# Places and order of the operand differences ahead of the MLP, and of one weight sum at the start of its down projection, in a hybrid SSD/attention layer

## The chip, the core and the metric

The kernel runs on one core of a Trainium2 chip. The core has a matrix engine (TensorE; PE in the profile, with its weight loads as PEld), a vector engine (DVE), a scalar engine (ACT), GpSimd (POOL) and SyncE (SP), each with its own queue of instructions, taken in order. POOL and SP also issue DMAs. The metric is the device time of one launch in microseconds (us); less is better.

## The reference

The reference is one layer of a streaming encoder: an RMS norm, a combined input projection, a Mamba-2 SSD group and a forgetting-attention group, an output projection, and then an MLP. There are 1152 tokens of width 1024 (1024 of a prompt and 8 x 16 of running streams). The change bears on the MLP only, whose hidden width is 4096:

```python
def trunk_layer(x, conv_prev, ssm_prev, fox_fn, norm1_w, w_in, ...):
...
    x = x + jnp.einsum("ble,ed->bld", mix, w_out)
    h = rms_norm(x, norm2_w)
    x = x + jnp.einsum("blf,fd->bld", jnp.square(jax.nn.relu(jnp.einsum("bld,df->blf", h, w_up))), w_down)
    return x, (k, v, logf, ssm_state, conv_state)
```

## The kernel before

**Float32 by parts.** A float32 operand is split into a high part (a copy by ACT into the matmul's format) and a low part (operand minus high part, on DVE). One product is then three matmuls: high weight by high operand, high weight by low operand, low weight by high operand. Every operand thus costs one ACT and one DVE instruction before PE can use it. A buffer that holds both parts is a *place*; part A's places are called XA10 to XA71, part B's XB10 to XB71, by the operand's number (1, 2, 5, 6, 7, 3, 4) and a half (0 or 1).

**Strassen.** Most of the MLP multiplies 2 x 2 blocks with seven products instead of eight. A product takes a sum or difference of weight blocks (`weights`, from line 1203, which yields them in the order 1, 2, 5, 6, 7, 3, 4) and a sum or difference of operands (`operand`, line 1170). `s1` (line 1210) is the weight sum of product 5, `s2` (L1213) that of product 6, `a21` (L1215) the difference of product 7 and `a12` (L1217) that of product 3. `parts` (L1199 on ACT, L1200 on DVE) splits a weight. Weights arrive by DMA from SP (`raws`, L1192) in the three buffers `wraw` and the two `a22`; their parts lie in four buffers `w`.

**The up projection** (`mlp`): hidden blocks f = 0 and 1 are multiplied plainly by `up_plain`, here called the first and the second, while the operands of the others are still being made; f = 2 to 15 follow with seven products each (`up`), of 24 matmuls each. The second's weights lie in four places of part A that are not yet taken (XA51, XA61, XA70, XA71). `chain("B", ...)` makes B's first operands of the third token block; its last low part is `made_b`. Then `operand` forms the differences of operands 5, 6, 7 and 4 (L1178), eight for each part, in place in the buffers of the normed activations (x20, xh, xl, g3), and splits them (L1180 on ACT, L1181 on DVE). After their products, `up_plain` forms the Strassen combinations of its hidden values (`hidden_out`, L1253), which POOL puts to DRAM (`Hd`, L1250); they lie in `ts`, two places of part B.

**The down projection** (`mlp_down`) goes through 19 steps (q, a, b): output block q, hidden blocks a to b. Step 0 takes two hidden blocks (12 matmuls in a product), step 1 three (18) and step 2 four (24). The hidden operands come back from `Hd` by POOL's DMAs (L1393) and are split by `hidden_parts` (L1401 on ACT, L1402 on DVE): 28 of them are split for the first four steps, 14 of these (f = 0 and 1) ahead of step 0. Results leave PSUM (tiles D, four of them) through DVE additions at L1429 and, for some, a copy at L1449.

**What sets the order.** A scheduler orders each engine's instructions by a simulation with priorities. `keep_in_program_order` pins instructions: all pinned ones of an engine keep the order in which the program writes them. `issue_after(x)` only holds an instruction behind x. `later` shifts a priority. So the order of an engine's queue, and not the program text alone, decides what waits for what.

Of the kernel before, what the change touches and what calls it, by code (L numbers as in the profile page):

```python
# [6 lines left out]
F32 = mybir.dt.float32  # L7
BF16 = mybir.dt.bfloat16
F32R = mybir.dt.float32r
I32 = mybir.dt.int32  # L10
AF = mybir.ActivationFunctionType
ALU = mybir.AluOpType
# [33 lines left out]
XB = 1  # L46
# [3 lines left out]
ORDER = (1, 2, 5, 6, 7, 3, 4)  # L50
# [13 lines left out]
class Trunk:  # L64
# [1098 lines left out]
        return [self.place(part, i, j, F32R) for j in range(2)]  # L1163

    def place(self, part, i, j, dt):
        return self.t(self.xap if part == "A" else self.xbp, [P, 2, 2, TC], dt, f"X{part}{i or 4}{j}")

    def operand(self, part, i, X):


        nc = self.nc
        b11, b12 = self.pieces(part, 0, 0), self.pieces(part, 0, 1)
        b21, b22 = self.pieces(part, 1, 0), self.pieces(part, 1, 1)
        src, minus = {1: (b11, None), 2: (b21, None), 0: (b12, None), 3: (b22, None),
                      5: (b11, (b12, b11)), 6: (b11, (b22, b11)), 7: (b12, (b22, b12)), 4: (b21, (b21, b11))}[i]
        for j in range(2):
            if minus is not None:
                self.tc.keep_in_program_order(nc.vector.tensor_tensor(src[j], minus[0][j], minus[1][j], op=ALU.subtract))  # L1178
            hi, lo = X[j][:, 0], X[j][:, 1]
            nc.scalar.activation(hi, src[j], AF.Copy)  # L1180
            nc.vector.tensor_tensor(lo, src[j], hi.bitcast(F32), op=ALU.subtract)  # L1181
# [18 lines left out]
        nc.vector.tensor_tensor(w[:, 1, 0:n], src, w[:, 0, 0:n].bitcast(F32), op=ALU.subtract)  # L1200
        return w

    def weights(self, load, n, raw=None, pin=lambda x: x):

        a11, a12, a21, a22 = self.raws(load, n, raw)
        v = self.nc.vector
        yield 1, self.parts(a11, n)
        yield 2, self.parts(a12, n)
        s1 = self.t(self.wr2, [P, 512], F32, "s1", 1)[:, 0:n]
        pin(v.tensor_tensor(s1, a21, a22, op=ALU.add))  # L1210
        yield 5, self.parts(s1, n)
        s2 = self.t(self.wr2, [P, 512], F32, "s2", 1)[:, 0:n]
        v.tensor_tensor(s2, s1, a11, op=ALU.subtract)  # L1213
        yield 6, self.parts(s2, n)
        pin(v.tensor_tensor(a21, a11, a21, op=ALU.subtract))  # L1215
        yield 7, self.parts(a21, n)
        v.tensor_tensor(a12, a12, s2, op=ALU.subtract)  # L1217
        yield 3, self.parts(a12, n)
        yield 4, self.parts(a22, n)
# [51 lines left out]
    def up_plain(self, f, A, B):  # L1271

        nc, I = self.nc, self.I
        halves = lambda part, i, dt: [self.place(part, i, j, dt) for j in range(2)]
        hb = [x[:, j] for x in halves("B", (6, 7)[f], F32) for j in range(2)]
        if f:
            ws = [x.rearrange("p a b t -> p (a b t)")[:, 0:1024].rearrange("p (a b) -> p a b", a=2)
                  for x in [self.place("A", i, 1, F32R) for i in (5, 6)] + halves("A", 7, F32R)]
        else:
            ws = [None] * 4  # L1280
        a = [self.parts(x, 512, w) for x, w in zip(self.raws(lambda ij: I["wu"][f, ij], 512, plain=True), ws)]
        for part, X in enumerate((A, B)):
            if f:
                groups = (((0, 0), (0, 1)), ((1, 0), (1, 1)))
            else:
                groups = (((0, 0), (1, 0)), ((0, 1), (1, 1)))
            for group in groups:
                banks = self.bank2()

                order = [(n, half, j) for half in range(2) for j in range(2) for n in range(2)]  # L1290
                if f:
                    order.sort()
                for n, half, j in order:
                    row, col = group[n]
                    ps = banks[:, n, 0:TC]
                    w, x = a[2 * row + half], X[((1, 2), (0, 3))[col][half]][j]
                    for k in range(2):
                        o = slice((2 * j + k) * P, (2 * j + k + 1) * P)
                        self.mm(ps, w[:, 0, o], x[:, 0, k], half == j == k == 0, False)
                        self.mm(ps, w[:, 0, o], x[:, 1, k], False, False)  # L1300
                        self.mm(ps, w[:, 1, o], x[:, 0, k], False, half == j == k == 1)
                    if half == j == 1:
                        h = hb[2 * row + col][:, part]
                        nc.scalar.activation(h, ps, AF.Relu)
                        nc.scalar.activation(h, h, AF.Square)
            yield
        ts = [x[:, j] for x in halves("B", 5, F32) for j in range(2)]
        for n in (0, 3, 1, 2):
            self.hidden_out(f, hb, ts, n)
        yield  # L1310
# [45 lines left out]
    def mlp(self):  # L1356
        XA, XB = self.XA, {}
        self.XB = XB
        self.late = []
        for i in (1, 2, 0, 3):  # L1360
            XB[i] = self.block("B", i)
        first, second = (self.up_plain(f, XA, XB) for f in range(2))
        next(first)
        next(second)
        with self.later(-1010000):
            rb, = self.norm2((2,))
            made_b = self.chain("B", ((2, (1, 2)),), {2: rb}, XB)
        for ins, tbs in ((self.made_a, (0, 1)), (made_b, (2,))):
            with self.tc.issue_after(ins.ins):
                for tb in tbs:  # L1370
                    self.scaled_rest(tb, self.room[:, tb, TB:TB + TB - TC] if tb < 2 else rb[:, TC:TB])
        for i in (0, 3):
            self.operand("B", i, XB[i])
        next(first)
        next(first)
        next(second)
        for i in (5, 6, 4, 7):
            XA[i] = self.block("A", i)
            self.operand("A", i, XA[i])
        next(second)  # L1380
        for i in (5, 6, 7, 4):
            XB[i] = self.block("B", i)
            self.operand("B", i, XB[i])
        for f in range(NC, NF):
            self.up(f)
# [9 lines left out]
    def hidden_parts(self, f, i):  # L1395

        nc = self.nc
        self.parted.add((f, i))
        h = self.hs[f, i]
        raw = h[:, 1].bitcast(F32)  # L1400
        nc.scalar.activation(h[:, 0], raw, AF.Copy)  # L1401
        nc.vector.tensor_tensor(h[:, 1], raw, h[:, 0].bitcast(F32), op=ALU.subtract)  # L1402

    def yrows(self, q, x):

# [72 lines left out]
        self.strassen(lambda ij: self.I["wd"][q, ij, :, ks], len(fs), rhs, ev, after, raw, **kw)  # L1478

    def mlp_down(self):  # L1480
        self.hs = {}
        steps = [(0, 0, 1), (1, 0, 2), (2, 0, 3), (3, 0, 3), (0, 2, 4), (1, 3, 5), (2, 4, 6), (3, 4, 7), (0, 5, 8), (1, 6, 9),
                 (2, 7, 10), (3, 8, 11), (0, 9, 12), (1, 10, 12), (2, 11, 13), (3, 12, 15), (0, 13, 15), (2, 14, 15), (1, 13, 15)]
        end = {f: n for n, (q, a, b) in enumerate(steps) for f in range(a, b + 1)}
        nc = self.nc
# [29 lines left out]
        for n, (q, a, b) in enumerate(steps):  # L1515
            def after(i):
                wait.append([])
                for f in range(NF - 4):
                    if end[f] == n:
                        self.hidden(f + 4, i)  # L1520
                        wait[-1].append((f + 4, i))
                if len(wait) > 4:
                    coming.extend(wait.pop(0))
                coming.sort(key=lambda fi: (begin[fi[0]], ORDER.index(fi[1])))
                for _ in range(2 if len(coming) > 3 else 1):
                    if coming:
                        self.hidden_parts(*coming.pop(0))

            kw = {}
            if n in (1, 2):  # L1530

                kw["pin"] = self.tc.keep_in_program_order
            if n == 1:
                kw["pre"] = lambda: self.load_y(1, nc.sync)
            self.down(q, list(range(a, b + 1)), n < 4, b == NF - 1, after, **kw)

# [250 lines left out]
```

## Time and profile before

| | us |
|---|---|
| three runs | 1685.35, 1692.79, 1697.54 |
| median | 1692.79 |
| the profiled execution, its own time | 1687.61 |
| its span in the trace | 1685.9 |

The busy shares in the page are 94% for PE, 75% for DVE, 47% for ACT and 29% for POOL. The MLP takes the time from about 955 us to the end of the span. In the views, a row gives a group of like instructions: start and duration in us, engine, line, operation, output and inputs, and their count; a bracket at its end is the engine's idle time ahead of the group, and what ended it. DMA issues are rows of the engine that issues them. Line numbers are those of the kernel before.

### The profile page before, as it was taken

The numbers are of one execution on the slowest core, as the hardware profiler recorded it, in microseconds if no ns is written. First come the engines' busy times: TensorE is split into PE (matmuls) and PEld (weight loads), VectorE is DVE, ScalarE is ACT, GpSimd is POOL, SyncE is SP. The second block draws the span as 40 slices with busy tenths as digits, with TensorE's granted clock in tenths as the row PEclk, the third lists the DMA queues.
The fourth block names the chain that finished last, engine by engine and source line by source line (L and its number), as shares of the span: only waits on it lengthen the run. The fifth ranks groups of instructions, "written<-read, shape, count | busy, mean of one in ns | idle before, by whom it ended". The sixth has DMA issues, their size and how long they took to land.

```text
span 1685.9 us, 29655 instructions
## 1 busy us (share of the span) xinstructions
PE 1591.1 (94%) x10709; PEld 1493.9 (89%) x10709; DVE 1262.4 (75%) x2336; ACT 788.9 (47%) x1573; POOL 483.9 (29%) x624
## 2 busy tenths in 40 slices
PE   8999999999898988999799989999999789999999
PEld 7999987889776867889689989999999689999998
DVE  7955676777777888795768787666668769888887
ACT  6322244446654444565754455445556224343431
POOL 1333322113654576333112012222225312111100
PEclk9999999999999999999999999999999899999999
DMA  7374477857889778965545244444447435344433
GB/s 232 100 206 118 117 216 249 288 161 216 258 265 285 211 246 254 295 188 161 162 159 167 69 138 154 144 149 149 143 143 273 153 98 181 114 142 140 148 119 105
DMA packets 193450, 299.75 MB, mean 178 GB/s; under 512 B 25592, under 2 KB 116520, under 8 KB 191256
## 3 DMA queue, kind: packets, MB, share of 16 engines
q1 hardware_dynamic: 133960, 183.60, 35.3%
q0 software_dynamic: 24240, 86.21, 15.7%
q10 hardware_dynamic: 35104, 28.06, 5.2%
q8 instruction: 85, 1.39, 0.3%
q14 instruction: 61, 0.50, 0.1%
HBM read 207.16 MB, written 90.63 MB: 177 GB/s over the span
## 4 chain that ended last, share of the span: by engine, by line
PE 67%; DMA 13%; DVE 12%; issue 3%; ACT 2%; SPq 2%; POOL 1%; ACTq 0%; DVEq 0%; POOLq 0%
PE D L127 41%; PE d L127 12%; PE o L127 4%; PE s L127 4%; PE c L127 2%; PE u L127 1%; DMA sb<-in_ssT 1%; DMA xb<-xbD 1%; DMA M<-acsTd 1%; DMA kt<-in_ckT 1%; DMA qb<-QS 1%; PE m L127 1%; DVE eh L702 1%; DVE qkv L305 1%; DMA wraw<-in_wq 1%
## 5 line engine op out<-in xcount | busy, mean ns | idle before, releaser
L127 PE MATMUL D<-XA,w 128*128 128x288 f32 x2616 | 404.4, 299 | 19.3 <-ACT w L1199 14.6
L127 PE MATMUL D<-XB,w 128*128 128x288 f32 x2616 | 399.5, 297 | 6.3 <-DVE XB L1181 4.0
L127 PEld LDWEIGHTS D<-XA,w 128*128 128x128 f32 x2616 | 369.3, 191 | 23.0 <-ACT w L1199 15.5
L127 PE MATMUL d<-xh,w 128*128 128x384 f32 x1344 | 370.9, 346 | 8.2 <-ACT xh L1003 2.6
L127 PEld LDWEIGHTS D<-XB,w 128*128 128x128 f32 x2616 | 366.6, 190 | 8.9 <-DVE XB L1181 4.7
L127 PEld LDWEIGHTS d<-xh,w 128*128 128x128 f32 x1344 | 245.9, 191 | 25.3 <-issue 10.1
L127 PE MATMUL d<-xl,w 128*128 128x384 f32 x672 | 231.7, 345 | 3.9 <-DVE xl L1004 3.7
L1199 ACT ACTIVATE w<-wraw 128x512 fp32r<-128x512 f32 (+2 forms) x132 | 78.4, 596 | 143.8 <-PE D L127 113.6
L123 POOL TENSOR_TENSOR w<-wraw,w 128x512 fp32r<-128x512 f32 x76 | 102.1, 1350 | 128.6 <-ACT w L121 125.0
L127 PEld LDWEIGHTS d<-xl,w 128*128 128x128 f32 x672 | 128.3, 191 | 11.9 <-DVE xl L1004 7.1
L121 ACT ACTIVATE w<-wraw 128x512 fp32r<-128x512 f32 x120 | 74.3, 627 | 93.5 <-PE d L127 50.3
L1200 DVE TENSOR_TENSOR w<-wraw,w 128x512 fp32r<-128x512 f32 (+2 forms) x132 | 84.6, 643 | 18.1 <-ACT w L1199 17.8
L1393 POOL DMA_DIRECT2D XA<-Hd x56 | 30.4, 542 | 166.3 <-PE D L127 128.4
L1199 ACT ACTIVATE w<-s 128x512 fp32r<-128x512 f32 (+2 forms) x66 | 39.0, 591 | 66.4 <-PE D L127 59.4
L1401 ACT ACTIVATE XB<-XB 128x576 fp32r<-128x576 f32 x56 | 37.9, 684 | 62.9 <-DMA XB<-Hd 62.6
L1401 ACT ACTIVATE XA<-XA 128x576 fp32r<-128x576 f32 x56 | 37.9, 683 | 52.0 <-DMA XA<-Hd 51.8
L127 PE MATMUL d<-wq,xh 128*128 128x384 f32 (+1 forms) x192 | 52.8, 351 | 7.5 <-ACT wq L121 6.7
L1402 DVE TENSOR_TENSOR XB<-XB 128x576 fp32r<-128x576 f32 x56 | 41.7, 751 | 21.7 <-ACT XB L1401 21.6
L1393 POOL DMA_DIRECT2D XB<-Hd x56 | 30.3, 541 | 91.1 <-PE D L127 70.4
L523 DVE SCALAR_TENSOR_TENSOR acc<-xr,cwh,acc 128x1024 f32<-128x1024 f32 x36 | 47.2, 1310 | 10.2 <-ACT acc L520 10.1
L127 PE MATMUL o<-wq,xh 128*128 128x384 f32 (+1 forms) x192 | 52.2, 347 | 0.0
L127 PE MATMUL s<-wq,xh 128*128 128x384 f32 (+1 forms) x192 | 52.1, 349 | 0.0
(572 smaller groups left out, 3223.5 us busy)
## 6 DMA issues: line engine op xcount, KB each, us to landing
Hd<-xl POOLq DMA_DIRECT2D x56, 288.0 KB, 4.3
XA<-Hd POOLq DMA_DIRECT2D x56, 288.0 KB, 3.3
XB<-Hd POOLq DMA_DIRECT2D x56, 288.0 KB, 3.7
wraw<-in_wch SPq DMA_DIRECT2D x56, 256.0 KB
wraw<-in_wu SPq DMA_DIRECT2D x50, 256.0 KB
wraw<-in_wos SPq DMA_DIRECT2D x48, 256.0 KB
M<-acsTd SPq DMA_DIRECT2D x18, 512.0 KB
kt<-in_ckT SPq DMA_DIRECT2D x8, 1024.0 KB
```

What stands on the lines that cost most here:

```text
L121: nc.scalar.activation(w[:, 0, :], raw, AF.Copy)
L123: eng.tensor_tensor(w[:, 1, :], raw, w[:, 0, :].bitcast(F32), op=ALU.subtract)
L127: self.nc.tensor.matmul(out, lhsT, rhs, start=start, stop=stop)
L305: nc.vector.tensor_tensor(v4, v4, rs[:, i, :].unsqueeze(2).to_broadcast([P, 4, 64]), op=ALU.mult)
L523: nc.vector.scalar_tensor_tensor(acc[:, 0:SEQ], xr[:, k:k + SEQ], cw[:, b, k:k + 1], acc[:, 0:SEQ], op0=ALU.mult, op1=ALU.add)
L702: nc.vector.tensor_tensor(eh[:, 1, w], ps[:, w], eh[:, 0, w].bitcast(F32), op=ALU.subtract)
L1199: nc.scalar.activation(w[:, 0, 0:n], src, AF.Copy)
L1200: nc.vector.tensor_tensor(w[:, 1, 0:n], src, w[:, 0, 0:n].bitcast(F32), op=ALU.subtract)
L1393: self.nc.gpsimd.dma_start(h[:, 1].bitcast(F32), self.Hd[f][:, (1, 2, 3, 5, 6, 7, 4).index(i)])
L1401: nc.scalar.activation(h[:, 0], raw, AF.Copy)
L1402: nc.vector.tensor_tensor(h[:, 1], raw, h[:, 0].bitcast(F32), op=ALU.subtract)
```

## The change

Four edits, none of which adds or takes away an instruction:

1. `place` crosses the places of part A's operands 5 and 6: operand 5 takes XA50 and XA60, operand 6 takes XA51 and XA61. The second's weights stay in XA51, XA61, XA70 and XA71.
2. The sixteen differences of `operand` are no longer pinned; each is only held behind `made_b`.
3. The second's `ts` are XB60 and XB61 instead of XB50 and XB51 (the first's `ts` stay in XB50 and XB51).
4. The sum `s1` and the difference `a21` of down steps 1 and 2 are no longer pinned. In step 1, `s1` is held behind the fourteenth low part of the hidden operands (`h_lo[13]`).

```diff
     def place(self, part, i, j, dt):
+        if part == "A" and i in (5, 6):
+
+            i, j = 5 + j, i - 5
         return self.t(self.xap if part == "A" else self.xbp, [P, 2, 2, TC], dt, f"X{part}{i or 4}{j}")
...
-                self.tc.keep_in_program_order(nc.vector.tensor_tensor(src[j], minus[0][j], minus[1][j], op=ALU.subtract))
+                with self.tc.issue_after(self.made_b.ins):
+                    nc.vector.tensor_tensor(src[j], minus[0][j], minus[1][j], op=ALU.subtract)
...
-    def weights(self, load, n, raw=None, pin=lambda x: x):
+    def weights(self, load, n, raw=None, behind=None):
...
-        pin(v.tensor_tensor(s1, a21, a22, op=ALU.add))
+        with ExitStack() as es:
+            if behind is not None:
+                es.enter_context(self.tc.issue_after(behind))
+            v.tensor_tensor(s1, a21, a22, op=ALU.add)
...
-        pin(v.tensor_tensor(a21, a11, a21, op=ALU.subtract))
+        v.tensor_tensor(a21, a11, a21, op=ALU.subtract)
...
-                  for x in [self.place("A", i, 1, F32R) for i in (5, 6)] + halves("A", 7, F32R)]
+                  for x in halves("A", 6, F32R) + halves("A", 7, F32R)]
...
-        ts = [x[:, j] for x in halves("B", 5, F32) for j in range(2)]
+        ts = [x[:, j] for x in halves("B", 5 + f, F32) for j in range(2)]
...
-            made_b = self.chain("B", ((2, (1, 2)),), {2: rb}, XB)
+            self.made_b = self.chain("B", ((2, (1, 2)),), {2: rb}, XB)
...
-        nc.vector.tensor_tensor(h[:, 1], raw, h[:, 0].bitcast(F32), op=ALU.subtract)
+        self.h_lo.append(nc.vector.tensor_tensor(h[:, 1], raw, h[:, 0].bitcast(F32), op=ALU.subtract))
...
-            if n in (1, 2):
-
-                kw["pin"] = self.tc.keep_in_program_order
             if n == 1:
+
+                kw["behind"] = self.h_lo[2 * len(ORDER) - 1].ins
                 kw["pre"] = lambda: self.load_y(1, nc.sync)
```

The changed file numbers its lines up to seven higher: L1178, L1181, L1200, L1210, L1213, L1215, L1217, L1253, L1320, L1402 and L1429 of before are L1182, L1185, L1204, L1217, L1220, L1222, L1224, L1260, L1327, L1409 and L1436 there; ACT's L1199, L1401 and L1449 are L1203, L1408 and L1456.

The instructions differ in order in two stretches only. The first is the start of the MLP. On DVE before, ahead of the first differences (x_1686 is x20; w_10750 and the next are the weights of f = 2; XB_1846 and XB_1847 are the first's ts in XB50 and XB51, XB_1858 is half of the second's; XA_1850 is the first half of operand 5):

```order
L1200 TENSOR_TENSOR w_10750<-wraw_10742,w_10750 128x512
L1200 TENSOR_TENSOR w_10780<-wraw_10744,w_10780 128x512
L1217 TENSOR_TENSOR wraw_10744<-wraw_10744,s_1884_10843 128x512
L1200 TENSOR_TENSOR w_10814<-s_1881_10812,w_10814 128x512
L1253 TENSOR_TENSOR XB_1846_10541<-XB_1812_10100 128x576
L1200 TENSOR_TENSOR w_10845<-s_1884_10843,w_10845 128x512
L1253 TENSOR_TENSOR XB_1846_10541<-XB_1813_10101,XB_1846_10541 128x576
L1253 TENSOR_TENSOR XB_1847_10542<-XB_1813_10101,XB_1812_10100 128x576
L1253 TENSOR_TENSOR XB_1847_10542<-XB_1813_10101,XB_1846_10541 128x576
L1178 TENSOR_TENSOR x_1686_9390<-xh_1601_8786,x_1686_9390 128x2x288
L1253 TENSOR_TENSOR XB_1858_10692<-XB_1824_10228 128x576
L1181 TENSOR_TENSOR XA_1850_10660<-x_1686_9390,XA_1850_10660 128x576
```

And the same place on DVE now, up to the same weight's low part (XB_1808 to XB_1811 are the last of B's plain operands, xl, xh and g are sources of differences):

```order
L1182 TENSOR_TENSOR xl_1602_8787<-g_1687_9391,xl_1602_8787 128x2x288
L1182 TENSOR_TENSOR xl_1603_8788<-g_1687_9391,xl_1603_8788 128x2x288
L1185 TENSOR_TENSOR XB_1808_10096<-g_1687_9391,XB_1808_10096 128x576
L1185 TENSOR_TENSOR XB_1809_10097<-g_1687_9391,XB_1809_10097 128x576
L1185 TENSOR_TENSOR XB_1810_10098<-g_1687_9391,XB_1810_10098 128x576
L1182 TENSOR_TENSOR xh_1601_8786<-xh_1601_8786 128x2x288 x2
L1185 TENSOR_TENSOR XB_1811_10099<-g_1687_9391,XB_1811_10099 128x576
L1185 TENSOR_TENSOR XA_1850_10660<-x_1686_9390,XA_1850_10660 128x576
L1185 TENSOR_TENSOR XA_1851_10661<-x_1686_9390,XA_1851_10661 128x576
L1182 TENSOR_TENSOR g_1687_9391<-g_1687_9391 128x576 x2
L1182 TENSOR_TENSOR x_1686_9390<-xh_1601_8786,x_1686_9390 128x2x288 x2
L1204 TENSOR_TENSOR w_10750<-wraw_10742,w_10750 128x512
```

Differences, and both low parts of operand 5 in part A, now stand ahead of the weights of f = 2; the differences used to begin behind the first's combinations.

The second stretch is the start of the down projection. On DVE before, around the sum of step 1 (XA_2251, XB_2252 and XB_2253 are the last of the 28 hidden operands; D_14447 and D_14473 are results of step 1; s_2281 is s1, s_2284 is s2; w_14495 and w_14520 are their parts):

```order
L1402 TENSOR_TENSOR XA_2251_14219<-XA_2251_14219 128x576
L1429 TENSOR_TENSOR x_2219_14147<-D_14447,x_2219_14147 128x576
L1402 TENSOR_TENSOR XB_2252_14221<-XB_2252_14221 128x576
L1402 TENSOR_TENSOR XB_2253_14223<-XB_2253_14223 128x576
L1429 TENSOR_TENSOR x_2219_14147<-D_14473,x_2219_14147 128x576
L1210 TENSOR_TENSOR s_2281_14493<-wraw_14432,a_2276_14434 128x384
L1213 TENSOR_TENSOR s_2284_14518<-s_2281_14493,wraw_14428 128x384
L1200 TENSOR_TENSOR w_14495<-s_2281_14493,w_14495 128x384
L1217 TENSOR_TENSOR wraw_14430<-wraw_14430,s_2284_14518 128x384
L1200 TENSOR_TENSOR w_14520<-s_2284_14518,w_14520 128x384
L1429 TENSOR_TENSOR x_2219_14147<-D_14498,x_2219_14147 128x2x576
L1429 TENSOR_TENSOR x_2219_14147<-D_14523,x_2219_14147 128x576
```

On DVE now, the place of the sum:

```order
L1436 TENSOR_TENSOR a_2225_14153<-D_14347,a_2225_14153 128x576
L1409 TENSOR_TENSOR XA_2239_14188<-XA_2239_14188 128x576
L1217 TENSOR_TENSOR s_2281_14493<-wraw_14432,a_2276_14434 128x384
L1409 TENSOR_TENSOR XB_2240_14197<-XB_2240_14197 128x576
L1409 TENSOR_TENSOR XB_2241_14199<-XB_2241_14199 128x576
L1204 TENSOR_TENSOR w_14436<-wraw_14428,w_14436 128x384
```

And on DVE now, what follows from the low part of w_14495 on:

```order
L1409 TENSOR_TENSOR XA_2250_14217<-XA_2250_14217 128x576
L1204 TENSOR_TENSOR w_14495<-s_2281_14493,w_14495 128x384
L1220 TENSOR_TENSOR s_2284_14518<-s_2281_14493,wraw_14428 128x384
L1409 TENSOR_TENSOR XA_2251_14219<-XA_2251_14219 128x576
L1436 TENSOR_TENSOR g_2218_14146<-D_14412,g_2218_14146 128x576
L1436 TENSOR_TENSOR x_2219_14147<-D_14447,x_2219_14147 128x576
L1222 TENSOR_TENSOR wraw_14432<-wraw_14428,wraw_14432 128x384
L1409 TENSOR_TENSOR XB_2252_14221<-XB_2252_14221 128x576
L1409 TENSOR_TENSOR XB_2253_14223<-XB_2253_14223 128x576
L1224 TENSOR_TENSOR wraw_14430<-wraw_14430,s_2284_14518 128x384
L1204 TENSOR_TENSOR w_14520<-s_2284_14518,w_14520 128x384
```

The sum has moved ahead of fourteen hidden low parts, directly behind the one of XA_2239, and its own low part ahead of the last three; the difference of product 7 (L1222) has moved ahead of two of them.

On ACT before, the high part of the sum stands behind all 28 copies and one result:

```order
L1401 ACTIVATE XA_2250_14217<-XA_2250_14217 128x576
L1401 ACTIVATE XA_2251_14219<-XA_2251_14219 128x576
L1401 ACTIVATE XB_2252_14221<-XB_2252_14221 128x576
L1401 ACTIVATE XB_2253_14223<-XB_2253_14223 128x576
L1449 ACTIVATE x_2219_14147<-D_14447 128x576
L1199 ACTIVATE w_14495<-s_2281_14493 128x384
L1199 ACTIVATE w_14520<-s_2284_14518 128x384
```

On ACT now:

```order
L1408 ACTIVATE XB_2249_14215<-XB_2249_14215 128x576
L1203 ACTIVATE w_14495<-s_2281_14493 128x384
L1408 ACTIVATE XA_2250_14217<-XA_2250_14217 128x576
L1408 ACTIVATE XA_2251_14219<-XA_2251_14219 128x576
L1408 ACTIVATE XB_2252_14221<-XB_2252_14221 128x576
L1408 ACTIVATE XB_2253_14223<-XB_2253_14223 128x576
L1203 ACTIVATE w_14520<-s_2284_14518 128x384
```

It stands ahead of the last four copies now, and the high part of w_14520 ahead of the result's copy.

More of the change, by code (lines that the diff above doesn't have):

```diff
@@ L1366, in mlp @@
             rb, = self.norm2((2,))
-            made_b = self.chain("B", ((2, (1, 2)),), {2: rb}, XB)
-        for ins, tbs in ((self.made_a, (0, 1)), (made_b, (2,))):
+            self.made_b = self.chain("B", ((2, (1, 2)),), {2: rb}, XB)
+        for ins, tbs in ((self.made_a, (0, 1)), (self.made_b, (2,))):
             with self.tc.issue_after(ins.ins):
@@ L1480, in mlp_down @@
     def mlp_down(self):
-        self.hs = {}
+        self.hs, self.h_lo = {}, []
         steps = [(0, 0, 1), (1, 0, 2), (2, 0, 3), (3, 0, 3), (0, 2, 4), (1, 3, 5), (2, 4, 6), (3, 4, 7), (0, 5, 8), (1, 6, 9),
```

## The prediction

> **What bounds the kernel now.** I read the span first, then the waits of PE, then busy time by stretches, and last the rows of the engines around the two stretches that the change reorders. Of the waits, grouped by what PE needed and what ended the wait (total us, times, longest), and of the busy time (stretch, length, then PE, PEld, DVE, ACT and POOL busy; then granted clock, DMA share, GB/s), these rows matter:
>
> ```profile
> span 1685.9 us, 29655 instructions
> PE D L127 <- ACT w L1199: 14.6, 4, 8.0
> PE D L127 <- DVE XB L1181: 4.0, 3, 2.9
> 985.00:1000.00 15.00, 10.31 (x45) 8.45 (x45) 14.83 (x23) 8.78 (x15) 0.74 (x1) 0.77 0.24 75
> 1320.00:1340.00 20.00, 11.84 (x61) 11.39 (x62) 12.91 (x21) 4.31 (x8) 1.58 (x3) 0.75 0.27 89
> 1360.00:1380.00 20.00, 17.83 (x121) 17.38 (x121) 12.56 (x18) 5.49 (x9) 1.10 (x2) 0.91 0.26 80
> 1380.00:1480.00 100.00, 100.00 (x756) 100.00 (x755) 88.51 (x138) 43.73 (x74) 19.37 (x36) 1.00 0.51 157
> ```
>
> PE is the bound: from 1380 to 1480 it is busy all the time at full clock. Time is lost where PE stands, and in the stretch at a lower granted clock behind it: 1320 to 1340 has 61 matmul records where 100 us at full pace have 756. Both places are the ones reordered, so the change is priced as PE time given back there. After either place PE runs full, so that what is saved stays saved, unless it is lost inside the place.
>
> **First stretch, start of the MLP (edits 1 to 3).** PE's rows:
>
> ```profile
> 982.35 2.69 PE L127 MATMUL D<-XA,w 128*128 128x288 f32 x19
> 988.43 0.40 PE L127 MATMUL D<-XB,w 128*128 128x288 f32 x1 [0.46 <-ACT XB L1180]
> 991.70 1.99 PE L127 MATMUL D<-XB,w 128*128 128x288 f32 x6 [2.87 <-DVE XB L1181]
> 994.37 1.57 PE L127 MATMUL D<-XB,w 128*128 128x288 f32 x5 [0.68 <-DVE XB L1181]
> 995.89 3.26 PE L127 MATMUL D<-XA,w 128*128 128x288 f32 x13
> 1010.11 1.77 PE L127 MATMUL D<-XA,w 128*128 128x288 f32 x12
> 1295.41 1.75 PE L127 MATMUL D<-XB,w 128*128 128x288 f32 x12
> 1297.00 1.76 PE L127 MATMUL D<-XA,w 128*128 128x288 f32 x12
> ```
>
> Full pace is the step from 1295.41 to 1297.00: 1.59 us for 12 matmuls, 0.1325 each. Product 5 of f = 2 begins at 982.35, product 5 of f = 3 at 1010.11; between them lie seven products of 24, 168 matmuls, worth 22.3 us. It takes 27.8, so 5.5 us are lost: the waits for part B's operands, and 13 matmuls in 3.26 us at low clock behind them. Why the operands are late shows on DVE:
>
> ```profile
> 963.71 1.49 DVE L1200 TENSOR_TENSOR w<-wraw,w 128x512 fp32r<-128x512 f32 x2 [5.18 <-ACT w L1199]
> 973.78 0.75 DVE L1178 TENSOR_TENSOR x<-xh,x 128x576 f32<-128x576 f32 x1
> 980.28 1.43 DVE L1253 TENSOR_TENSOR XB<-XB,XB 128x576 f32<-128x576 f32 x2 [0.72 <-ACT XB L1305]
> 990.89 0.75 DVE L1181 TENSOR_TENSOR XB<-xl,XB 128x576 fp32r<-128x576 f32 x1
> 993.57 0.75 DVE L1181 TENSOR_TENSOR XB<-xl,XB 128x576 fp32r<-128x576 f32 x1
> ```
>
> DVE stands for 5.18 us ahead of 963.71, waiting for a weight, and starts the sixteen differences only at 973.78. They are pinned to one another in alternation with low parts that wait for places held by the second's weights, so the low parts of XB51 and XB60 come at 990.89 and 993.57. In the changed order eight differences and both low parts of operand 5 in part A stand in that idle time: ten instructions of 0.67 us each (two in a train take 1.43, one 0.75) from 958.53, where the idle time begins, to 965.2. So the first weight's low part is 1.5 us later than at 963.71; its product lies 72 matmuls, 9.5 us, ahead of 982.35, which hides that. From 965.2 to the end of the low part of XB50 lie 13 instructions of 0.67 and six on weights of 0.75: 978.4, or about 981 if a combination waits for ACT as at 980.28. PE wants that part 12 matmuls into product 5, at 983.9.
>
> Edit 3 moves the second's combinations to XB60 and XB61, so that operand 6 of part B now waits for their way to DRAM, which operand 5 did before. Of the DMAs in 960 to 1000, and of those in the crowded stretch from 1270 to 1325 (KB each, median us from issue to landing), with POOL's last issue before:
>
> ```profile
> Hd<-XB POOLq DMA_DIRECT2D x13, 288.0 KB, 2.4
> XB<-Hd POOLq DMA_DIRECT2D x14, 288.0 KB, 7.0
> 984.01 0.54 POOL L1250 DMA_DIRECT2D Hd<-XB  x1 [1.46 <-DVE XB L1253]
> ```
>
> The last combination, issued at 984.01 before, ends five instructions of 0.67 and one of 0.75 behind 980.28, with its own 0.67 at 985.1; issued in 0.54 it goes out by 985.8 and lands at 988.2. PE wants the high part of XB61 about 92 matmuls after 982.35, at 994.5. Even a landing of 7.0 us leaves a margin of about one us after ACT's copy. So the whole loss of 5.5 us is taken as gain. The ends: 5.5, if nothing is late; and a loss of 2.5, if the landing takes twice the 7.0 and PE stands some 6.5 us, with 1.5 us of slow matmuls behind. I take 5.5, since the nearest row, of these same puts, is 2.4. PE's own reordered rows ahead of 982.35 and two weight loads that move on SP behind the copies of residual rows are covered by the same margins.
>
> **Second stretch, start of the down projection (edit 4).** PE, DVE, ACT and SP:
>
> ```profile
> 1315.51 2.39 PE L127 MATMUL D<-XB,w 128*128 128x288 f32 x16 [0.43 <-DVE w L1200]
> 1325.94 4.44 PE L127 MATMUL D<-XA,w 128*128 128x288 f32 x18 [8.04 <-ACT w L1199]
> 1330.22 0.97 PE L127 MATMUL D<-XB,w 128*128 128x288 f32 x6
> 1335.00 0.53 PE L127 MATMUL D<-XA,w 128*128 128x288 f32 x2 [2.22 <-ACT w L1199]
> 1352.68 0.53 PE L127 MATMUL D<-XA,w 128*128 128x288 f32 x2 [2.17 <-ACT w L1199]
> 1353.40 1.81 PE L127 MATMUL D<-XA,w 128*128 128x288 f32 x7 [0.20 <-DVE w L1200]
> 1363.47 0.53 PE L127 MATMUL D<-XA,w 128*128 128x288 f32 x2 [2.17 <-ACT w L1199]
> 1371.69 1.37 PE L127 MATMUL D<-XA,w 128*128 128x288 f32 x9
> 1309.83 0.75 DVE L1402 TENSOR_TENSOR XA<-XA 128x576 fp32r<-128x576 f32 x1
> 1320.05 0.75 DVE L1402 TENSOR_TENSOR XA<-XA 128x576 fp32r<-128x576 f32 x1
> 1324.72 0.55 DVE L1210 TENSOR_TENSOR s<-wraw,a 128x384 f32<-128x384 f32 x1
> 1325.92 0.56 DVE L1200 TENSOR_TENSOR w<-s,w 128x384 fp32r<-128x384 f32 x1
> 1333.49 0.55 DVE L1215 TENSOR_TENSOR wraw<-wraw,wraw 128x384 f32<-128x384 f32 x1
> 1309.65 1.25 ACT L1401 ACTIVATE XB<-XB 128x576 fp32r<-128x576 f32 x2
> 1337.16 0.63 ACT L1199 ACTIVATE w<-wraw 128x512 fp32r<-128x512 f32 x1 [1.39 <-DMA wraw<-in_wd]
> 1288.67 0.37 SPq L1192 DMA_DIRECT2D a<-in_wd  x1
> 1334.10 2.27 SPq L1192 DMA_DIRECT2D wraw<-in_wd  x3
> ```
>
> From the down projection's first product at 1297.00 to the last product of step 2 at 1371.69 lie 7 x 12, 7 x 18 and 6 x 24 = 354 matmuls, worth 46.9 us; it takes 74.7, so 27.8 us are lost. The sum of step 1 stands behind all hidden low parts, at 1324.72, and PE waits 8.04 us for its high part. Behind it 18 matmuls take 4.28 us, to 1330.22 (0.238 each, the low clock). The difference of product 7 waits for a result at 1333.49, and that frees the buffers of step 2's weights, so SP issues them at 1334.10, ACT has the first at 1337.16, and step 2 has two waits of 2.17 us of its own with slow matmuls behind them.
>
> In the changed order the sum is directly behind the low part at 1309.83, thus at 1310.50; it takes 0.47 and makes all behind it that much later (PE reaches product 5 at 1317.90 + 0.47 = 1318.4; 1317.90 is 1325.94 less the wait). ACT copies its high part behind the two copies begun at 1309.65, by 1311.6. Its low part stands behind the low part at 1320.05, which ends at 1320.72, or 1321.2 with the 0.47; it is there at 1321.8. PE does two matmuls, stands for about 3.2 us, and does the other 16 at 0.238: 1325.6. The low part of product 6's weight has ahead of it s2, three more instructions of 0.67, the difference of product 7 (0.47), the last two hidden low parts (1.34) and that of product 3 (0.47): it is there at 1327.0, 0.9 us after PE's second matmul of product 6. Everything else of step 1 is then on DVE ahead of PE, so that 70 matmuls run to 1336.3. Step 2's raw weights are issued when the difference of product 7 and the last uses of the buffers are through, at about 1325 to 1330, and land some three us later (1334.10 to 1337.16 before); its sum's parts are wanted at 1342.7. So step 2 runs through: 144 matmuls, to 1355.4. The gain is 1371.69 - 1355.4 = 16.3 us. The ends: 22.3, if PE never stands from 1318.4 on (234 matmuls, to 1349.4); 4.7, if only the low part is earlier (1325.92 less 1321.2) and the later waits return. I take 16.3, since the later waits hang on the issue at 1334.10, which does move.
>
> How long the clock stays low is open. The row at 1353.40 has 7 matmuls in 1.6 us, 0.23 each, behind a wait of 2.17 us, and at 1371.69 the pace is full again; I let the 16 matmuls behind the wait be slow and no later ones. The Trainium skill, "TensorE: Matmul & The Clock Gate", section "Part 1: The HAM clock gate (the "warmup" mystery)", has the clock fall to half after an idle window of about 3.4 us and return after about 3.4 us of sustained work. By that rule the break of 0.9 us at 1326.1 could start the second count anew, an estimate of 14 more slow matmuls, 1.5 us, and the gain here would be 14.8 instead of 16.3. The trace bears out a low clock behind a wait, but already behind 2.17 us and not only 3.4; no row shows a count begun anew, and the sum goes by the rows.
>
> **The sum.** 5.5 + 16.3 = 21.8 us. From the profiled execution's 1687.61 that gives 1665.8; this execution is 5.2 below the median of the three runs, from which it gives 1671.0. I forecast the middle, 1668.
>
> **The rivals.**
> *Only the second stretch pays.* The first stall returns as a wait for the places XB60 and XB61, or for another operand of part B. For it: DVE has almost no slack from 980 on (14.83 of 15 us busy from 985). Against it: the margins above. The gain is 16.3, the time about 1674.
> *The sum is early but its stall moves.* The low part of the sum, of s2 and of the next weights still share DVE's queue with hidden parts and results; if step 2's waits return, 4.7 remain of the second stretch: 5.5 + 4.7 = 10.2, the time about 1680. For it: DVE is without a gap there, and the walk rests on 20 instructions. Against it: the loads' issue moves.
> *The sum blocks DVE.* If the raw block issued at 1288.67 has not landed by 1310.50, DVE's queue stands with 14 low parts behind it, 1 us for each us. It decides against the kernel from 1310.50 + 21.8 = 1332.3 on, 43.6 us after the issue; a landing at 1350 would give 1708. The highest median landing above is 7.0 us, so that is unlikely.
> *The change doesn't do what it says*: DVE's order does differ as shown, so that is left with the rest.
>
> **How the numbers follow.** The forecast has 0.62, the first rival 0.12, the second 0.18, the blocking one 0.04, others 0.04. The runs before spread from 1685 to 1698, so the forecast alone has 1662 to 1674; the low end with all 27.8 us saved is 1662, and 1660 with some of that spread; the second rival asks for 1682. About 1% (17 us) is what a measurement can tell from no change. Faster by over 1%: nine tenths of the forecast's 0.62 and half of the first rival's 0.12, so 0.62. Within 1%: the rest of these, the second rival and others, 0.34. Slower: 0.04.
>
> **What would show it.** In the profile after, product 5 of f = 2 and that of f = 3 lie 22.3 us apart, with no wait of over 0.5 us for XB at L1185. The wait for the sum's weight is 3 to 4 us and ends on DVE's low part (L1204) instead of ACT's high one; step 2's loads, at 1334.10 before, go out some 5 us sooner against the first down product or more, and the waits of 2.2 us are gone. A wait of DVE at the sum's line L1217, or one for Hd of ACT at XB60 or XB61, would show the forecast wrong.

## The result, and the profile after

The changed kernel takes 1666.9 us in the median of four runs (1664.36 to 1667.09), against 1691.78 us of the kernel before (1685.35 to 1697.54): a ratio of 0.985 with a 95% interval of 0.9813 to 0.9888, 24.9 us less. The forecast was 1668 us.

The profiled spans differ by less than that, 1685.9 against 1665.4 us. The rows that divide them: the span and PE's wait for a cached key block of the changed kernel, then, of DVE, the last low part of the plain operands (L1144) and the first addition of a down result (L1429, L1436 in the changed file). Of the kernel before:

```profile
952.42 1.60 DVE L1144 TENSOR_TENSOR XB<-xl,XB 128x576 fp32r<-128x576 f32 x2
1300.55 0.75 DVE L1429 TENSOR_TENSOR g<-D,g 128x576 f32<-128x576 f32 x1
```

Of the changed kernel, with PE's row first:

```profile
span 1665.4 us, 29671 instructions
328.95 1.94 PE L127 MATMUL s<-kt,qb 128*32 128x512 f32 x8 [3.17 <-DMA kt<-in_ckT]
957.29 1.60 DVE L1144 TENSOR_TENSOR XB<-xl,XB 128x576 fp32r<-128x576 f32 x2
1296.54 0.75 DVE L1436 TENSOR_TENSOR g<-D,g 128x576 f32<-128x576 f32 x1
```

Up to the last low part the changed kernel is 4.9 us *later*, in code that the change does not touch: PE waits 3.17 us for a key block there, and the kernel before shows no such wait in its profile. Over the twelve profiles of this document that low part begins anywhere from 947.8 to 965.5 us, so runs and spans move by up to 17.7 us before the MLP begins. Two differences are free of it and are used from here on: the *first stretch*, from that low part to the first addition, 1300.55 - 952.42 = 348.1 us before and 339.3 after, and the *second stretch*, from the addition to the end of the span, 385.4 before and 368.9 after. The gains are 8.9 and 16.5 us, 25.4 together, close to the 24.9 of the medians.

PE's rows in the first stretch of the changed kernel, then DVE's:

```profile
987.19 1.75 PE L127 MATMUL D<-XA,w 128*128 128x288 f32 x12
1003.49 1.88 PE L127 MATMUL D<-XA,w 128*128 128x288 f32 x12 [0.20 <-DVE x L1327]
1009.97 1.75 PE L127 MATMUL D<-XA,w 128*128 128x288 f32 x12
960.64 1.42 DVE L1182 TENSOR_TENSOR x<-xh,x 128x576 f32<-128x576 f32 x2
967.33 1.42 DVE L1185 TENSOR_TENSOR XA<-x,XA 128x576 fp32r<-128x576 f32 x2
971.34 1.28 DVE L1204 TENSOR_TENSOR w<-wraw,w 128x512 fp32r<-128x512 f32 x2
984.81 0.75 DVE L1185 TENSOR_TENSOR XB<-xl,XB 128x576 fp32r<-128x576 f32 x1
990.88 0.75 DVE L1260 TENSOR_TENSOR XB<-XB,XB 128x576 f32<-128x576 f32 x1
```

Product 5 of f = 2 begins at 987.19 and that of f = 3 at 1009.97, 22.8 us apart for 168 matmuls, with one wait of 0.20 us. The differences begin at 960.64, ahead of the first weight's low part at 971.34, and DVE has no idle time there. The low part of XB50 is there at 985.6, 3.2 us ahead of PE (12 matmuls behind 987.19). The row at 990.88 is the second's last combination.

PE, DVE and SP in the second stretch of the changed kernel, with its waits of PE from 840 us on first:

```profile
PE D L127 <- DVE w L1204: 6.7, 6, 3.2
1292.99 1.76 PE L127 MATMUL D<-XA,w 128*128 128x288 f32 x12
1314.20 0.42 PE L127 MATMUL D<-XA,w 128*128 128x288 f32 x2
1317.79 3.84 PE L127 MATMUL D<-XA,w 128*128 128x288 f32 x16 [3.17 <-DVE w L1204]
1321.46 0.43 PE L127 MATMUL D<-XB,w 128*128 128x288 f32 x2
1322.99 0.80 PE L127 MATMUL D<-XB,w 128*128 128x288 f32 x4 [0.84 <-DVE w L1204]
1351.24 1.36 PE L127 MATMUL D<-XA,w 128*128 128x288 f32 x9
1306.50 0.54 DVE L1217 TENSOR_TENSOR s<-wraw,a 128x384 f32<-128x384 f32 x1
1317.19 0.54 DVE L1204 TENSOR_TENSOR w<-s,w 128x384 fp32r<-128x384 f32 x1
1320.13 0.54 DVE L1222 TENSOR_TENSOR wraw<-wraw,wraw 128x384 f32<-128x384 f32 x1
1284.64 0.39 SPq L1196 DMA_DIRECT2D a<-in_wd  x1
1320.73 5.43 SPq L1196 DMA_DIRECT2D wraw<-in_wd  x3
```

The waits for ACT's high part, 14.6 us before, are gone. PE stands once for 3.17 us, for the low part of the sum's weight, does 16 matmuls at low clock in 3.67 us (1317.79 to 1321.46, 0.23 each), stands 0.84 us more for the next low part, and runs from there. The last product of step 2, at 1371.69 before, begins at 1351.24. Step 2's loads go out at 1320.73, and step 2 has no wait.

### The profile page after: what moved, and what is told of

Its sections match the earlier page's. It is cut to its first block, busy times and chain, and to the rows that moved or that the text cites. A ratio compares the mean times of both kernels' runs of the same rounds, so it can differ in the third digit from the quotient of the medians.

```text
span 1665.4 us, 29671 instructions
## 1 busy us (share of the span) xinstructions
PE 1584.9 (95%) x10709; PEld 1491.8 (90%) x10709; DVE 1262.4 (76%) x2336; ACT 788.5 (47%) x1573; POOL 484.1 (29%) x624
## 3 DMA queue, kind: packets, MB, share of 16 engines
q8 instruction: 85, 1.39, 0.3%
## 4 chain that ended last, share of the span: by engine, by line
PE 51%; DMA 8%; DVE 7%; issue 4%; ACT 1%; POOL 1%; SPq 0%; ACTq 0%; DVEq 0%; POOLq 0%
PE D L127 38%; PE d L127 6%; PE o L127 2%; PE s L127 1%; DMA XB<-Hd 1%; PE u L127 1%; DMA sb<-in_ssT 1%; PE c L127 1%; DVE eh L702 1%; DVE xl L974 1%; DMA wraw<-in_wos 1%; PE m L127 1%; DMA out_sssm<-sb 1%; DMA z<-zD 1%; DVE z L999 1%
## 5 line engine op out<-in xcount | busy, mean ns | idle before, releaser
L127 PE MATMUL D<-XA,w 128*128 128x288 f32 x2616 | 398.4, 296 | 8.1 <-DVE w L1204 4.1
L127 PE MATMUL D<-XB,w 128*128 128x288 f32 x2616 | 394.7, 295 | 2.6 <-DVE w L1204 2.6
L127 PEld LDWEIGHTS D<-XA,w 128*128 128x128 f32 x2616 | 364.5, 189 | 10.5 <-DVE w L1204 4.6
L1203 ACT ACTIVATE w<-wraw 128x512 fp32r<-128x512 f32 (+2 forms) x132 | 78.8, 597 | 134.3 <-PE D L127 128.0
L1204 DVE TENSOR_TENSOR w<-wraw,w 128x512 fp32r<-128x512 f32 (+2 forms) x132 | 84.7, 642 | 10.2 <-ACT w L1203 10.1
L1203 ACT ACTIVATE w<-s 128x512 fp32r<-128x512 f32 (+2 forms) x66 | 39.1, 593 | 75.5 <-PE D L127 63.9
L1408 ACT ACTIVATE XB<-XB 128x576 fp32r<-128x576 f32 x56 | 37.7, 683 | 63.5 <-DMA XB<-Hd 63.4
L1408 ACT ACTIVATE XA<-XA 128x576 fp32r<-128x576 f32 x56 | 37.9, 682 | 49.0 <-DMA XA<-Hd 48.8
L1409 DVE TENSOR_TENSOR XB<-XB 128x576 fp32r<-128x576 f32 x56 | 41.7, 751 | 20.6 <-ACT XB L1408 20.3
```

The lines of the kernel that those rows point to most:

```text
L127: self.nc.tensor.matmul(out, lhsT, rhs, start=start, stop=stop)
L1203: nc.scalar.activation(w[:, 0, 0:n], src, AF.Copy)
L1409: self.h_lo.append(nc.vector.tensor_tensor(h[:, 1], raw, h[:, 0].bitcast(F32), op=ALU.subtract))
```

## The experiments

For each: first and second stretch as above (before 348.1 and 385.4; changed 339.3 and 368.9), and the time against runs of the kernel before on the same chip. Between profiles of the same code at that place the first stretch repeats to 0.2 us, and the second of the changed code to 0.4; of the old code it moved by 1.5 (e1 below). The times move by more, so the stretches decide. The diffs are against the changed kernel, that of e2 against the kernel before; `...` stands for lines left out.

| run | first | second | sum | median us | ratio, 95% interval |
|---|---|---|---|---|---|
| before | 348.1 | 385.4 | 733.5 | 1691.78 | |
| changed | 339.3 | 368.9 | 708.1 | 1666.9 | 0.985 (0.9813 to 0.9888) |
| e9, changed again | 339.3 | 369.0 | 708.3 | 1668.22 | 0.9856 (0.9821 to 0.989) |
| e1, edits 1 to 3 | 339.3 | 383.8 | 723.1 | 1680.81 | 0.9921 (0.9898 to 0.9944) |
| e2, edit 4 | 347.9 | 368.9 | 716.8 | 1676.46 | 0.9895 (0.9863 to 0.9927) |
| e3, pins kept | 348.2 | 368.9 | 717.0 | 1677.86 | 0.9909 (0.9875 to 0.9943) |
| e5, not crossed | 339.3 | 368.8 | 708.1 | 1664.92 | 0.9841 (0.9806 to 0.9877) |
| e8, no places moved | 339.6 | 369.2 | 708.8 | 1666.57 | 0.9847 (0.9812 to 0.9882) |
| e6, no hold | 346.7 | 366.1 | 712.7 | 1672.42 | 0.9872 (0.983 to 0.9914) |
| e11, hold at the 21st | 339.3 | 372.4 | 711.7 | 1672.77 | 0.9881 (0.9832 to 0.9929) |
| e7, f = 3 behind product 7 | 339.3 | 366.9 | 706.2 | 1668.88 | 0.9856 (0.9829 to 0.9884) |
| e10, f = 3 behind product 3 | 339.3 | 364.5 | 703.8 | 1664.34 | 0.9831 (0.9798 to 0.9865) |

### e1: edits 1 to 3 alone

```diff
-    def weights(self, load, n, raw=None, behind=None):
+    def weights(self, load, n, raw=None, pin=lambda x: x):
...
-            v.tensor_tensor(s1, a21, a22, op=ALU.add)
+        pin(v.tensor_tensor(s1, a21, a22, op=ALU.add))
...
-        v.tensor_tensor(a21, a11, a21, op=ALU.subtract)
+        pin(v.tensor_tensor(a21, a11, a21, op=ALU.subtract))
...
+                kw["pin"] = self.tc.keep_in_program_order
...
-                kw["behind"] = self.h_lo[2 * len(ORDER) - 1].ins
```

> Edits 1 to 3 alone; the sum and the difference of steps 1 and 2 are pinned as before. Theory (the two stretches are independent, and the first is worth what the profile after shows between its last low part at L1144 and the first down product, 344.6 us before and 335.7 after): 8.9 us below before, about 1683, ratio 0.995, with the 8.04 us wait for the sum's weight still there and 74.7 us from the first down product to the last product of step 2. Rival (the prediction's own term): 5.5 us, about 1686, ratio 0.997. Second rival (the edits help only together): no gain.

The first stretch has the whole gain, 8.9 us. The waits of PE from 960 to 1400 us show what is left:

```profile
PE D L127 <- ACT w L1203: 14.6, 4, 8.3
```

Those are the old waits, for the sum and in step 2. The ratio lies a little below the 0.995 expected, with an interval that ends at 0.9944. Of that, 1.5 us lie in the second stretch, and the clock explains them. Before, PE's wait of 2.22 us at 1335.00 is followed by 3.4 us at half clock, and the next 38 matmuls take 6.8 us (to 1341.83). In e1 the same wait is 1.93 us, at 1339.78; the clock stays full, and the 38 take 5.3 us (to 1345.06). The rest is of the size by which the part ahead of the MLP moves between runs.

### e2: edit 4 alone

```diff
-        pin(v.tensor_tensor(s1, a21, a22, op=ALU.add))
+        with ExitStack() as es:
+            if behind is not None:
+                es.enter_context(self.tc.issue_after(behind))
+            v.tensor_tensor(s1, a21, a22, op=ALU.add)
...
-        pin(v.tensor_tensor(a21, a11, a21, op=ALU.subtract))
+        v.tensor_tensor(a21, a11, a21, op=ALU.subtract)
...
-                kw["pin"] = self.tc.keep_in_program_order
...
+                kw["behind"] = self.h_lo[2 * len(ORDER) - 1].ins
```

> Edit 4 alone; places, pins of the differences and ts as before. Theory: 16.4 us below before, about 1675, ratio 0.990; from the first down product to the last product of step 2 58.3 us instead of 74.7; the first stretch stays at 344.6 us. Rival (part of the 16.4 comes from the first stretch having moved DMA and POOL work): under 13 us, ratio over 0.992.

The second stretch is that of the changed kernel to 0.1 us, the first that of before. The two halves of the change are independent of one another: e1 saves 8.9 us in the first stretch and e2 16.5 in the second, the 25.4 of the whole. The sums of e1 and e2, 10.4 and 16.7 us less, come to 27.1 only by the 1.5 us of the clock in e1.

### e3: the pins of the differences kept

```diff
-                with self.tc.issue_after(self.made_b.ins):
-                    nc.vector.tensor_tensor(src[j], minus[0][j], minus[1][j], op=ALU.subtract)
+                self.tc.keep_in_program_order(nc.vector.tensor_tensor(src[j], minus[0][j], minus[1][j], op=ALU.subtract))
```

> The changed kernel with the sixteen differences pinned again in program order; crossed places, second's ts and the sum stay as changed. Theory (the pins, and not the places, kept the differences from DVE's idle time): the first stretch is back at about 344.6 us, the time at about 1676. Rival (the places are what held the low parts): the first stretch keeps most of its gain, 336 to 339 us, the time under 1671.

PE's waits from 950 to 1400 us:

```profile
PE D L127 <- DVE w L1203: 6.4, 6, 3.2
PE D L127 <- DVE XB L1184: 3.9, 3, 2.8
```

The waits for XB are those of the kernel before (4.0 us in three), though the places are as changed. The pins alone cost the first stretch its 8.9 us.

### e5 and e8: the places as before

```diff
-        if part == "A" and i in (5, 6):
-
-            i, j = 5 + j, i - 5
...
-                  for x in halves("A", 6, F32R) + halves("A", 7, F32R)]
+                  for x in [self.place("A", i, 1, F32R) for i in (5, 6)] + halves("A", 7, F32R)]
```

That is e5; e8 has besides:

```diff
-        ts = [x[:, j] for x in halves("B", 5 + f, F32) for j in range(2)]
+        ts = [x[:, j] for x in halves("B", 5, F32) for j in range(2)]
```

> The changed kernel with part A's operands 5 and 6 on XA50, XA51 and XA60, XA61 again; everything else as changed. Read in the trace: from DVE's last low part at L1144 to the first addition of a down result, 348.1 us before and 339.3 in the changed kernel. Theory (the pins alone cost the stretch, and without them the scheduler finds other work for DVE until XA51 is free): 339 to 341 us. Rival (DVE stands at the low part of XA51 until the second's weight there is used up): 342 us or more. The rest of the span stays at 368.9 us.

> The changed kernel with both moves of places undone: operands 5 and 6 not crossed, the second's ts in XB50 and XB51. Of the edits to the first stretch only the removed pins are left. Theory (pins alone): 339 to 342 us from the last low part at L1144 to the first addition of a down result. Rival (operand 5 of part B, now behind the second's way to DRAM, stalls PE): 343 us or more, with a wait of PE for XB at the low part's line.

Both rivals fall. Without the crossing nothing is lost, and without either move of places the first stretch is 0.4 us longer and PE never waits for XB in it. Once the pins are gone the scheduler finds other work: in the profile of e8, PE does 38 matmuls of part A in a row from 981.71, where the changed kernel has 12 from 987.19. Edits 1 and 3 bring at most 0.4 us.

### e6: no hold on the sum

```diff
-                kw["behind"] = self.h_lo[2 * len(ORDER) - 1].ins
```

> The changed kernel without the hold behind the fourteenth low part: DVE's order has the sum about 15 us earlier, some 6.5 us after SP issues its last weight block, and its low part ahead of three more hidden low parts. Theory of the blocked queue: the block has not landed, DVE stands at the sum for 2 to 8 us with the hidden low parts behind it, and the kernel is 1 to 7 us slower than the changed one (1668 to 1674). Rival (the block lands in about 7 us as the median of the transfers around it): no stand over 1 us, the low part comes 2 us earlier, and the kernel is 1 to 3 us faster than the changed one (about 1665).

Of DVE, SP and PE:

```profile
1281.36 0.41 DVE L1204 TENSOR_TENSOR w<-s,w 128x256 fp32r<-128x256 f32 x1
1290.04 0.56 DVE L1217 TENSOR_TENSOR s<-wraw,a 128x384 f32<-128x384 f32 x1 [8.26 <-issue]
1275.16 0.44 SPq L1196 DMA_DIRECT2D a<-in_wd  x1
1292.01 1.18 PE L127 MATMUL D<-XB,w 128*128 128x288 f32 x2 [3.55 <-DVE xh L1327]
1296.92 2.77 PE L127 MATMUL D<-XB,w 128*128 128x288 f32 x10 [3.73 <-DVE w L1204]
1313.69 2.39 PE L127 MATMUL D<-XA,w 128*128 128x288 f32 x16 [1.16 <-DVE w L1204]
```

DVE stands 8.26 us at the sum. The profile names no releaser ("issue"); the instruction reads only two weight blocks, the later issued at 1275.16. That it waited for the landing of that block, which then took up to 14.9 us, is so inferred and not seen. PE loses 3.55 and 3.73 us behind that, and gets back 2.8 us later, since the low part of the sum's weight now stands ahead of three more hidden low parts: a wait of 1.16 us instead of 3.17, no slow matmuls behind it, no wait of 0.84 us, and a new one of 1.51 us for a result. Together 4.6 us slower than the changed kernel. The hold is worth that.

### e11: the hold at the twenty-first low part

```diff
-                kw["behind"] = self.h_lo[2 * len(ORDER) - 1].ins
+                kw["behind"] = self.h_lo[3 * len(ORDER) - 1].ins
```

> The changed kernel with the sum of step 1 held behind the twenty-first hidden low part instead of the fourteenth; in DVE's order its low part then stands behind all 28, as before the change, while the pins of steps 1 and 2 stay removed. It tells the early sum from the removed pins. Theory (most of the 16.4 us come from the removed pins: the difference of product 7 no longer waits for a result, and step 2's loads go out early): the first wait is back at about 8.3 us, step 2 still runs without a wait, and from the first addition of a down result to the end it takes about 373 us (before 385.4, changed 368.9). Rival (the early sum is what pays): 380 us or more, with waits of 2.2 us in step 2.

Of PE, DVE and SP:

```profile
1318.13 0.53 PE L127 MATMUL D<-XA,w 128*128 128x288 f32 x2 [1.39 <-ACT w L1203]
1324.59 0.85 PE L127 MATMUL D<-XB,w 128*128 128x288 f32 x2 [5.93 <-ACT w L1203]
1323.84 0.55 DVE L1222 TENSOR_TENSOR wraw<-wraw,wraw 128x384 f32<-128x384 f32 x1
1324.45 3.31 SPq L1196 DMA_DIRECT2D wraw<-in_wd  x3
```

The old wait is back as 1.39 and 5.93 us, and the second stretch still takes only 372.4 us. So 13.0 of the 16.5 us come from the pins that are gone (385.4 to 372.4), and 3.5 from the early sum, each give or take the 1.5 us by which the clock moved this stretch in e1. Which pin counts is read from the rows: the difference of product 7, at 1323.84, comes 24.4 us behind the first addition (1299.40), 23.6 in the changed kernel and 32.9 before, and in all three step 2's loads go out 0.6 us behind it. No run takes away this pin alone.

### e7 and e10: the low parts of hidden block 3 held back

The last wait of 3.17 us is for a low part that stands behind low parts of f = 3, wanted first in step 2. e7 holds these seven behind the low part of product 7's weight, e10 behind that of product 3's; of step 1, `hidden_parts` is then called after products 7, 3 and 4 (e10: 3 and 4) alone, and in step 0 once behind each product. The core of e10:

```diff
+        with ExitStack() as es:
+            if f == 3:
+                es.enter_context(self.tc.issue_after(self.lo3.ins))
+            self.h_lo.append(nc.vector.tensor_tensor(h[:, 1], raw, h[:, 0].bitcast(F32), op=ALU.subtract))
...
-                for _ in range(2 if len(coming) > 3 else 1):
+                for _ in range(1 if n == 0 else 0 if n == 1 and i in (1, 2, 5, 6, 7) else 4 if n == 1 else 2 if len(coming) > 3 else 1):
```

> The changed kernel with the seven low parts of hidden block 3, first wanted in step 2, held behind the low part of product 7's weight in step 1. Theory (the 3.2 us wait left is the low part of the sum's weight standing behind low parts that nobody needs yet): that wait falls to about 1.3 us with no slow matmuls behind it, the 0.8 us wait goes, some 1 to 2 us come back as a wait for a PSUM bank released late; from the first addition of a down result to the end 364.5 to 367 us instead of 368.9, so 2 to 4.4 us faster than the changed kernel. Rival (the stall only moves to step 2, whose operands then come late): 368.5 us or more.

> The changed kernel with the seven low parts of hidden block 3 held behind the low part of product 3's weight in step 1, one product later than in the run that held them behind product 7's (that one: 366.9 us from the first addition of a down result to the end, with two waits of 1.0 and 0.8 us for a PSUM bank whose addition stood behind those low parts). Theory: the additions of products 2 and 5 now stand ahead of the low parts, both waits go, 365.0 to 365.5 us, 3.5 us less than the changed kernel. Rival (the low parts, now later, hold up step 2 or product 4's weight): 366.5 us or more.

PE in e7:

```profile
1320.48 2.40 PE L127 MATMUL D<-XA,w 128*128 128x288 f32 x16 [1.42 <-DVE w L1204]
1322.71 0.42 PE L127 MATMUL D<-XB,w 128*128 128x288 f32 x2
1328.66 0.50 PE L127 MATMUL D<-XB,w 128*128 128x288 f32 x2 [1.02 <-DVE x L1442]
1329.92 0.50 PE L127 MATMUL D<-XA,w 128*128 128x288 f32 x2 [0.77 <-DVE x L1442]
```

And PE in e10:

```profile
1314.29 2.40 PE L127 MATMUL D<-XA,w 128*128 128x288 f32 x16 [1.42 <-DVE w L1204]
1321.82 2.29 PE L127 MATMUL D<-XB,w 128*128 128x288 f32 x16
```

In e7 the wait falls to 1.42 us and is followed by matmuls at full pace, but 1.79 us come back as waits for additions that free PSUM: 2.0 us gained. In e10 they are gone, 364.5 us, 4.3 us less than the changed kernel. Its time is below that of the kernel before and of the changed one, yet its interval (0.9798 to 0.9865) overlaps that of the changed one: the gain over it is shown by the stretches, not by the times.

### e9: the changed kernel again

> The changed kernel once more, beside the others on the same chip. 339.3 and 368.9 us in the two stretches; the time at about 1667 if the part ahead of the MLP takes as long as in the earlier run, within 10 us otherwise.

The stretches repeat to 0.2 us. The span of this profile is 6.3 us longer (1671.7), and the part ahead of the MLP alone makes that up: its last low part begins at 963.42 instead of 957.29. The clock was another, though: behind the same wait of 3.17 us it was at half for 6.83 us, against 3.41 in the first profile of the same code (see "The clock" below).

## Why the prediction was right

**Second stretch.** The walk held at each step, with every time 4.0 us earlier: the sum at 1306.50 (forecast 1310.50), its low part there at 1317.73 (1321.8), PE behind the 16 slow matmuls at 1321.46 (1325.6), the next low part at 1322.94 (1327.0), the last product of step 2 at 1351.24 (1355.4). From the first down product at 1292.99 to 1351.24 it is 58.3 us, 16.4 us less than before, against 16.3 forecast. What the prediction could not part, e11 did: it spoke of the early sum first, but most of the gain hangs on the pins that are gone, and by the rows on that of product 7's difference and with it the issue of step 2's loads, for which the prediction had chosen 16.3 over 4.7.

**First stretch: a mis-sized term.** The forecast was 5.5 us, the runs show 8.9. The step that failed is "product 5 of f = 3 at 1010.11". These rows of the kernel before stand behind that one:

```profile
1011.72 2.42 PE L127 MATMUL D<-XB,w 128*128 128x288 f32 x17
1013.98 1.75 PE L127 MATMUL D<-XA,w 128*128 128x288 f32 x12
```

From 982.35 to 1010.11 PE's rows hold only 139 matmuls and not 168; with the 12 at 1010.11 and these 17 they are 168, so product 5 begins in the row at 1013.98. From 982.35 it is 31.6 us, so 9.4 us were lost, not 5.5. A row by its operand class, XA or XB, does not tell which product it is; the count would have shown it, and so would a check against the long stretch, since 1297.00 - 1010.11 is 286.9 us for matmuls that at 0.1325 take 283. The mechanism, idle DVE time that the pins kept closed, is what e3 shows. But the prediction put it down to three edits together; e8 shows that the unpinned differences do it and the places do not.

That 1668 came within 1.1 us of the median is in part luck: the sum was 21.8 us where the stretches gained 25.4, and the part ahead of the MLP moves the time by more than the difference.

**The margin of XB61.** It held. The last combination came later than forecast against product 5 (it ends at 991.6, 4.4 us behind the product's start at 987.19; forecast were 985.1, 2.7 us behind 982.35), and PE still never waited for XB in that stretch. Another count was off and did no harm: ahead of the first weight's low part at 971.34 stand ten differences and two low parts of operand 5, not eight and two, so that it comes 2.8 us later against the last low part of the plain operands (14.0 us behind it, 11.3 before) and not 1.5. The margin of 9.5 us hides that.

**The rivals.** That only one stretch pays was wrong by e1 and e2. The stall of the sum did not move into step 2, where PE has no wait. The blocked queue did not come about, but it was nearer than the prediction had it: e6 has the weight block take up to 14.9 us, if it is what DVE waited for, twice the 7.0 us taken for its bound. The sum runs 21.9 us behind the issue (1284.64 to 1306.50), so some 7 us of margin are left of that hold and not 15.

**The clock.** The sum by the trace's rows, 16.3 us, held: in the changed kernel the matmuls behind the wait of 0.84 us run at full pace at once (4 from 1322.99, and no further wait up to 1351.24), and no count begins anew. But it held in part by luck. These stretches, with PE's busy time, the granted clock, DMA share and GB/s, are of the changed kernel and then of e9, from 0.2 us and 0.1 us behind the start of the 16 matmuls on:

```profile
1318.00:1321.00 3.00, 3.00 (x13) 0.50 0.27 79
1321.00:1324.00 3.00, 2.16 (x16) 0.99 0.25 87
1324.00:1327.00 3.00, 3.00 (x13) 0.50 0.41 120
1327.00:1330.00 3.00, 2.96 (x14) 0.57 0.26 87
```

In e9 the same code has a half clock for 6.83 us, and some six more matmuls are slow. Its second stretch is only 0.2 us longer, since they fill the time in which PE stood for 0.84 us (0.24 are left of that); the 14.8 us of the prediction's other reading came about in neither. The kernel before has 6.83 us at half clock behind 991.70 as well, with a break of 0.68 us in it, so the prediction's "no row shows a count begun anew" goes further than its rows; whether a break does that stays open. The Trainium skill, "TensorE: Matmul & The Clock Gate", section "Part 1: The HAM clock gate (the "warmup" mystery)", has the clock return after one busy window or more of about 3.4 us. The profiles agree: from 940 to 1650 us, every stretch of half clock in the twelve of them lasts 3.41, 6.83 or 10.24 us, worked out from the granted clock in windows of 0.5 us.

## What to carry to other kernels

A pin that fixes the order of instructions which wait for different things turns each one's wait into everyone's; hold an instruction only behind what it must not overtake, and let the scheduler fill the idle time. An unheld instruction that waits for a DMA can go wrong the other way, blocking its engine's queue from a place that is too early. Price a stall from two positions that are the same instruction: count the matmuls between them, and check the pair against a longer stretch.

## What the runs showed of the hardware

The length of a wait alone does not tell whether the clock falls, nor for how long. From 940 to 1650 us, no wait of PE of up to 1.93 us (e1) was by itself followed by a half clock, and 16 matmuls behind waits of 1.16 us (e6) and 1.42 us (e7, e10) took 2.2 us, full pace; all waits of 2.17 us or more had one. But PE's wait for `sq` (L976) early in the kernel, 2.43 us in the kernel before, e10, e2 and e7, was followed by a half clock in the first two and by none in the others. And the half clock is not tied to the end of the wait: behind 3.17 us the changed kernel has it when PE goes on, e3 (3.16 us) 1.3 us later; it lasted 3.41 us in the changed kernel, e2, e3 and e5, and 6.83 us in e8 and e9.

A weight block of 192 KB, issued in a stretch in which the DMA engines moved 388 GB/s (e6, 1270 to 1290), took up to 14.9 us if it is what DVE waited for, while the median of the larger transfers around it was 6.7 and 6.9.
